# Modulation by chunks of features, streamed into four head tiles of the first projection

## The chip, the cores and the metric

The kernel runs on one core of one Trainium2 chip. The metric is the device time of one execution in microseconds (us); lower is better. The engines are named as in the profile: PE (TensorE, with PEld for its weight loads), DVE (VectorE), ACT (ScalarE), POOL (GpSimd) and SP (SyncE, which issues most DMAs).

## The reference, cut to what matters

Two networks run one after the other on 256 tokens of 1024 features, in float32. The change lies at the start of the first one, which has two layers. Each layer turns a conditioning vector into six modulation vectors (shift, scale and gate, twice), normalizes the tokens, shifts and scales them, projects them with `w_in` and attends in three kinds of heads:

```python
mod_x = (silu_c @ w_ada[l] + b_ada[l])[:, None, :]      # w_ada[l]: 1024 x 6144
mod_c = (silu_cc @ w_ada[l] + b_ada[l])[None, None, :]
sh1_x, sc1_x, gt1_x, sh2_x, sc2_x, gt2_x = jnp.split(mod_x, 6, axis=-1)
...
hx = modulate(rms_norm(x, g_norm1[l]), sh1_x, sc1_x)     # h * (1 + scale) + shift
hc = modulate(rms_norm(ctx, g_norm1[l]), sh1_c, sc1_c)
qa, ka, va, qb, kb, vb, qc, kc, vc = jnp.split(hx @ w_in[l], bounds, axis=-1)
...
oa, oa_t = mixer_a(...)   # grouped-query attention, rope
ob, ob_t = mixer_b(...)   # neighbourhood attention
oc, oc_t = mixer_c(...)   # differential attention, rope
x = x + gt1_x * (jnp.concatenate([oa, ob, oc], axis=-1) @ w_out[l])
```

The 256 context tokens go through the first layer beside the 256 tokens of `x`, so that a projection there has 512 columns. In the second layer the context only gives keys and values, and a query projection has 256 columns.

## The kernel before

Features lie on partitions, in eight chunks of 128 (`KC`), and tokens lie along the free dimension. A weight tile is 128 output features by all 1024 inputs, 512 KB. `weight` loads it into a `raw` buffer and splits it into `hi` (an ACT copy, L261) and `lo` (a DVE subtraction, L262); there are four buffers of each. A product of a chunk is three matmuls of 512 columns (`mm1`, L269 to L271), so that a projection tile is 24 matmuls. `gemm` runs the first tiles (its head, three of them) chunk by chunk side by side and the others one after the other. The accumulators are five PSUM banks (`mm`); three more (`at`) serve all else. `done` is called for each finished tile: for queries and keys it is the norm `qk` (a matmul at L450 with ACT and DVE work around it), for values a transpose (`values`, L468).

The modulation vectors come from `ada`, a generator. One step loads 512 KB of `w_ada` (128 inputs by one whole vector of 1024) into a `raw` buffer and adds it up with four matmuls (L372). Eight steps make a vector. `first` runs 16 steps, for the shift and scale of layer 0, before it loads the head's three weight tiles. After the eighth step come the norm's statistics (`stat_end`, L350 and L351, then the chain in `rsq`), and DVE multiplies the 16 half chunks of tokens with it (L820, L821). `mod_gain` (L413) makes the factors of all chunks at once, and `modulate` applies them: ACT writes the high part (L428), DVE the low one (L429, L430).

18 projection tiles follow in the order of `IN1`. `gemm` does the first six, three of them in its head. The other twelve are a generator, `project`. The attention calls `fill` once for each unit (a block of scores, its softmax and its transposes): it takes the next projection, or, when there is none left, an `ada` step for a later vector. The order of attention is c (differential), b (neighbourhood), a (grouped query). The framework sorts the instructions of each engine when the program is built; nothing is sorted on the chip.

Of the kernel before, what the change touches and what calls it, by code (L numbers as in the profile page):

```python
# [9 lines left out]
F32 = mybir.dt.float32  # L10
F32R = mybir.dt.float32r
# [27 lines left out]

_CON = [("ident", 128), ("ones", 128), ("ones128", 128), ("bd64", 128), ("bd32", 128), ("causal", 128)]  # L40
_COFF = {}
# [18 lines left out]
def _constants():  # L60
# [24 lines left out]
    put("winmask", np.where((kc[None] >= st[:, None]) & (kc[None] < st[:, None] + 16), 0.0, MASKED))  # L85
    put("causal", np.where(i[None, :] <= i[:, None], 0.0, MASKED))
    m = np.zeros((P, 8, P), np.float32)
    m[:, 0] = np.eye(P)
# [9 lines left out]
def prep(v):  # L98
# [13 lines left out]
    d["ccT"] = cc  # L112
    d["w_ada"] = f(v["w_ada"])

    def tiles(w):
# [70 lines left out]
class Kern:  # L186
# [91 lines left out]

    def gemm(self, tiles, done, head=3, hook=None, order=None, fill=None, ws=None):

# [135 lines left out]

    def modulate(self, l, v, gain, streams, zs, n, xn=None):

        nc = self.nc
        xs = []  # L420
        for c in range(KC):
            hi, lo = self.n(F32R), self.n(F32R)
            if xn:
                t = self.t()[:, :512]
                for part, _ in streams:
                    u = slice(part * 256, (part + 1) * 256)
                    g, sh = gain[:, c, part:part + 1], self.mod(l, v, c, part)
                    nc.scalar.activation(hi[:, u], xn[c][:, u], AF.Identity, scale=g, bias=sh)  # L428
                    nc.vector.tensor_scalar(t[:, u], xn[c][:, u], g, sh, ALU.mult, ALU.add)  # L429
                nc.vector.tensor_tensor(lo, t, hi.bitcast(F32), ALU.subtract)  # L430
                xs.append((hi, lo))
                continue
# [173 lines left out]
    def first_layer(self, l):  # L606
# [6 lines left out]
        both = ((0, X), (1, C))  # L613
        zs, head = None, self.head
        if not wc:
# [5 lines left out]
        cut = {n: [(h[:, :n], o[:, :n]) for h, o in xs] for n in (256, 512)}  # L621
        gains = {}
# [168 lines left out]
    def first(self, ctx):  # L791
# [19 lines left out]
        self.G1, self.G2 = {}, {}  # L811
        self.known, self.mods = -1, self.ada()
        for i in range(16):
            next(self.mods)
            if i == 7:
                with self.tc.issue_after(self.last_ada):
                    zs = [self.stat_end(s) for s in st]
                self.xn = [self.n() for _ in range(KC)]
                for c in range(KC):
                    nc.vector.tensor_tensor(self.xn[c][:, :256], self.H[:, c, TM:TH], zs[0], ALU.mult)  # L820
                    nc.vector.tensor_tensor(self.xn[c][:, 256:], self.C[:, c, :], zs[1], ALU.mult)  # L821
        self.head = [self.weight(A["w1_in"][0, j]) for j in range(3)]
        nc.sync.dma_start(self.CON1, A["con1"])
        nc.sync.dma_start(self.LAM, bass.AP(A["lamv"].tensor, 0, [[0, P], [1, 256]]))

# [465 lines left out]
def build(tc, A, out, dbg=None):  # L1291
    with ExitStack() as ctx:
# [7 lines left out]

_INS = ["hT", "cT", "ccT", "w_ada", "w1_in", "w1_out", "w1_up", "w1_dn", "w2_in", "w2_fg", "w2_out", "w2_up1", "w2_dn1",
        "w2_up2", "w2_dn2", "walpha", "vec", "lamv", "rpb", "con", "con1", "lmask"]
# [18 lines left out]
```

## Time and profile before

| | us |
|---|---|
| median of 3 runs | 2428.66 |
| fastest and slowest run | 2425.72, 2434.18 |
| the profiled execution's own time | 2433.39 |
| its span | 2431.6 |
| first projection matmul starts at | 43.10 |

Times in the rows are counted from the span's start. A row of a timeline gives start, duration, engine, line, operation, output<-input, count, and in brackets how long the engine was idle before and what ended that.

### The profile page before, as it was taken

What the parts mean: (1) busy time and instruction counts of PE and PEld (TensorE: products, weight loads), DVE (VectorE), ACT (ScalarE), POOL (GpSimd) and SP (SyncE); (2) the same over time, 40 slices, a digit from 0 to 9 for tenths busy, and PEclk for the clock granted to TensorE, in tenths of its full rate; (3) what the DMA queues carried; (4) which work ended last, traced back from release to release, by engine and by line L of the source; (5) the groups of instructions that cost most, each with busy time, mean ns of one, the idle gap of its engine ahead of it and who ended that gap; (6) DMA issues with size and microseconds to landing.
All of it is one profiled execution on the core that took longest, in us unless ns stands there. A gap on an engine that the chain in (4) does not pass through costs nothing. (4 is left out here: it accounts for less than half of the span.)

```text
span 2431.6 us, 40872 instructions
## 1 busy us (share of the span) xinstructions
PE 2320.8 (95%) x16128; PEld 2043.5 (84%) x16128; DVE 1523.2 (63%) x2605; ACT 1270.2 (52%) x2196; POOL 401.7 (17%) x417
## 2 busy tenths in 40 slices
PE   5999999999999989999999999899999999998998
PEld 3665677778877758999999988899989999888997
DVE  4667665444547776776664876676466557666664
ACT  3658644333346775664444545554454444466553
POOL 0300021000022001211111320321121122113111
PEclk8999999999999999999999999999999999999999
DMA  7313335433233246556555533445545545334653
GB/s 269 103 37 131 113 130 173 139 121 96 93 117 120 71 156 211 194 177 191 183 168 180 167 106 105 148 157 174 174 148 178 169 147 195 104 114 149 196 180 118
DMA packets 100993, 358.57 MB, mean 147 GB/s; under 512 B 11488, under 2 KB 12864, under 8 KB 100544
## 3 DMA queue, kind: packets, MB, share of 16 engines
q1 hardware_dynamic: 98640, 349.82, 44.4%
q0 software_dynamic: 1792, 5.53, 0.9%
q8 instruction: 127, 2.08, 0.4%
q10 hardware_dynamic: 368, 0.59, 0.1%
q14 instruction: 66, 0.54, 0.1%
HBM read 354.83 MB, written 1.07 MB: 146 GB/s over the span
## 5 line engine op out<-in xcount | busy, mean ns | idle before, releaser
L269 PE MATMUL mm_t<-n_t,hi_t 128*128 128x272 f32 (+2 forms) x3600 | 1112.4, 310 | 25.4 <-ACT n_t L839 18.7
L270 PE MATMUL mm_t<-n_t,hi_t 128*128 128x272 f32 (+2 forms) x3600 | 1109.5, 308 | 6.0 <-DVE n_t L840 5.0
L271 PE MATMUL mm_t<-n_t,lo_t 128*128 128x272 f32 (+2 forms) x3600 | 1106.0, 308 | 1.1 <-DVE lo_t L262 1.1
L262 DVE TENSOR_TENSOR lo_t<-raw_t,hi_t 128x1024 fp32r<-128x1024 f32 (+1 forms) x574 | 713.2, 1246 | 391.2 <-ACT hi_t L261 387.1
L261 ACT ACTIVATE hi_t<-raw_t 128x1024 fp32r<-128x1024 f32 (+1 forms) x574 | 595.5, 1039 | 680.6 <-PE mm_t L270 509.4
L269 PEld LDWEIGHTS mm_t<-n_t,hi_t 128*128 128x128 f32 x3600 | 686.0, 191 | 77.7 <-ACT n_t L839 20.9
L270 PEld LDWEIGHTS mm_t<-n_t,hi_t 128*128 128x128 f32 x3600 | 688.5, 191 | 38.1 <-DVE n_t L840 8.4
L271 PEld LDWEIGHTS mm_t<-n_t,lo_t 128*128 128x128 f32 x3600 | 687.9, 191 | 33.0 <-issue 5.8
L269 PE MATMUL mm_t<-q_t,hi_t 128*128 128x272 f32 (+2 forms) x896 | 274.6, 307 | 0.7 <-ACT q_t L306 0.7
L270 PE MATMUL mm_t<-q_t,hi_t 128*128 128x272 f32 (+2 forms) x896 | 274.4, 306 | 0.0
L271 PE MATMUL mm_t<-q_t,lo_t 128*128 128x272 f32 (+2 forms) x896 | 274.3, 306 | 0.0
L343 POOL TENSOR_TENSOR t_t<-t_t 128x272 f32<-128x272 f32 (+1 forms) x108 | 122.9, 1143 | 540.2 <-ACT t_t L339 515.2
L269 PEld LDWEIGHTS mm_t<-q_t,hi_t 128*128 128x128 f32 x896 | 168.4, 188 | 8.8 <-ACT q_t L306 1.1
L270 PEld LDWEIGHTS mm_t<-q_t,hi_t 128*128 128x128 f32 x896 | 168.9, 188 | 7.6 <-DVE q_t L307 0.2
L271 PEld LDWEIGHTS mm_t<-q_t,lo_t 128*128 128x128 f32 x896 | 168.9, 189 | 7.5
L888 POOL TENSOR_TENSOR t_t<-t_t 128x272 f32<-128x272 f32 (+1 forms) x88 | 75.6, 860 | 443.3 <-DVE t_t L882 386.9
L738 POOL TENSOR_TENSOR t_t<-t_t 128x512 f32<-128x512 f32 (+1 forms) x44 | 56.7, 1288 | 442.2 <-ACT t_t L737 442.2
L882 DVE TENSOR_TENSOR t_t<-mm_t,t_t 128x272 f32<-128x272 f32 (+1 forms) x176 | 75.6, 436 | 64.2 <-PE mm_t L271 62.4
L372 PE MATMUL at_t<-raw_t,CS 128*32 128x256 f32 x768 | 70.6, 431 | 35.7 <-DMA raw_t<-in_w_ada_dram 35.4
L307 DVE TENSOR_TENSOR q_t<-t_t,q_t 128x272 fp32r<-128x272 f32 (+2 forms) x112 | 55.8, 498 | 73.4 <-ACT q_t L306 73.4
L306 ACT ACTIVATE q_t<-t_t 128x272 fp32r<-128x272 f32 (+2 forms) x112 | 52.3, 467 | 90.4 <-POOL t_t L738 47.8
L480 ACT ACTIVATE t_t<-mm_t,s_t 128x512 f32<-128x512 f32 (+1 forms) x120 | 72.7, 607 | 26.5 <-DVE s_t L478 25.7
(253 smaller groups left out, 2146.9 us busy)
## 6 DMA issues: line engine op xcount, KB each, us to landing
raw_t<-in_w_up_dram SPq DMA_DIRECT2D x264, 512.0 KB, 3.3
raw_t<-in_w_in_dram SPq DMA_DIRECT2D x118, 512.0 KB, 3.4
raw_t<-in_w_ada_dram SPq DMA_DIRECT2D x96, 512.0 KB, 4.4
raw_t<-in_w_dn_dram SPq DMA_DIRECT2D x96, 448.0 KB, 3.3
raw_t<-in_w_dn_dram SPq DMA_DIRECT2D x48, 512.0 KB, 3.6
raw_t<-in_w_out_dram SPq DMA_DIRECT2D x32, 512.0 KB, 3.4
raw_t<-in_w_fg_dram SPq DMA_DIRECT2D x16, 512.0 KB, 3.3
q_t<-cum POOLq DMA_DIRECT2D x8, 272.0 KB, 7.4
```

The source lines that it names most:

```text
L261: nc.scalar.activation(hi[:, :k], raw[:, :k], AF.Copy)
L262: nc.vector.tensor_tensor(lo[:, :k], raw[:, :k], hi[:, :k].bitcast(F32), ALU.subtract)
L269: self.nc.tensor.matmul(ps, wh, xh, start=start, stop=False)
L270: self.nc.tensor.matmul(ps, wh, xl, start=False, stop=False)
L271: self.last_mm = self.nc.tensor.matmul(ps, wl, xh, start=False, stop=stop).ins
L307: self.nc.vector.tensor_tensor(lo, src, hi.bitcast(F32), ALU.subtract)
L343: st.eng.tensor_tensor(st.acc, st.acc, sq, ALU.add)
L372: self.last_ada = nc.tensor.matmul(ps[32 * g:32 * g + 32], self.CS[:, k, :], wv[:, g], start=k == 0, stop=k == KC - 1).ins
L480: nc.scalar.activation(pm[:, i * nk:(i + 1) * nk], sp[:, i * nk:(i + 1) * nk], AF.Exp, bias=m[:, i:i + 1], accum_out=sm[:, i:i + 1])
L738: nc.gpsimd.tensor_tensor(u, u, g, ALU.mult)
L882: nc.vector.tensor_tensor(u, ps, z[0], ALU.mult)
L888: nc.gpsimd.tensor_tensor(u, u, g, ALU.mult)
```

## The change

For layer 0 the shift and scale are no longer made as two whole vectors. The weights are packed again on the host (`w_ada0`) by chunks of 128 output features, each with its shift and scale columns together. `ada_chunk` loads a chunk in four DMAs of 256 KB into buffers of the `heads` pool (18 of them), adds up with eight matmuls (L433 of the changed kernel) and copies the sums to SBUF with ACT; `mod_chunk` adds the four partial sums with two small matmuls against a selector (L444), adds the bias, makes the gain of this chunk alone and writes its high and low part. `gemm` calls them through `feed`, so that the head's matmuls of chunk k follow chunk k's modulation. The head has four tiles, and their weights are loaded ahead of the modulation weights. The constants of rope and window are loaded after the last chunk, and the lambda vectors from ACT's queue. In both layers three more projections run before the first attention unit.

```diff
+    a = v["w_ada"][0, :, :2048].reshape(4, 2, P, 2, KC, P)
+    d["w_ada0"] = f(a.transpose(4, 0, 2, 1, 3, 5).reshape(KC, 4, P, 512))
...
         for i, k in enumerate(order):
+            if feed:
+                feed(k)
             for w, ps, t in zip(ws, pss, tiles):
                 self.mm1(ps, w, k, t[1][k], i == 0, i == KC - 1)
...
-        for l, v in ((l, v) for l in range(2) for v in range(6)):
+        for l, v in ((l, v) for l in range(2) for v in range(2 * (1 - l), 6)):
...
+    def ada_chunk(self, c):
+        nc = self.nc
+        ps = self.atp()[:, :256]
+        for h in range(2):
+            ws = [self.q()[:, :512] for _ in range(2)]
+            for i, w in enumerate(ws):
+                self.last_dma = nc.sync.dma_start(w, self.A["w_ada0"][c, 2 * h + i]).ins
+            for g in range(4):
+                self.last_ada = nc.tensor.matmul(ps[32 * g:32 * g + 32], self.CS[:, 4 * h + g, :],
+                                                 ws[g // 2][:, g % 2 * 256:(g % 2 + 1) * 256], start=h == 0, stop=h == 1).ins
+        e = self.t()[:, :256]
+        nc.scalar.activation(e, ps, AF.Copy)
+        return e
+
+    def mod_chunk(self, c, e):
+        nc = self.nc
+        m = self.atp()[:, :4].rearrange("p (v s) -> p v s", v=2)
+        for v in range(2):
+            nc.tensor.matmul(m[:, v], e[:, v * P:(v + 1) * P], self.con("sel"), start=v == 0, stop=v == 1)
+        o, _ = _VOFF["b_ada"]
+        for v in range(2):
+            nc.vector.tensor_scalar(self.MOD[0][:, v * KC + c], m[:, v], self.VEC[:, o + v * KC + c:o + v * KC + c + 1], None,
+                                    ALU.add)
+        gain = self.G1[0]
+        nc.vector.tensor_scalar(gain[:, c], self.MOD[0][:, KC + c], 1.0, self.gh[:, c:c + 1], ALU.add, ALU.mult)
...
-        xs = self.modulate(l, 0, self.G1[l], both, zs, 512, self.xn if wc else None)
+            def feed(k):
+                while len(sums) < min(k + 2, KC):
+                    sums.append(self.ada_chunk(len(sums)))
+                x = self.mod_chunk(k, sums[k])
...
-        self.gemm(tiles[:6], done, ws=head)
+        self.gemm(tiles[:6], done, ws=head, head=len(head), feed=feed,
+                  hook=late if wc else None)
...
+        for _ in range(3):
+            next(self.project)
         for j in range(2):
             po = self.attend(l, "c", get("qc", j), get("kc", j), get("vc", j), wc, lam=lam)
...
+        self.head = [self.weight(A["w1_in"][0, j]) for j in range(4)]
...
-        for i in range(16):
-            next(self.mods)
-            if i == 7:
-                with self.tc.issue_after(self.last_ada):
-                    zs = [self.stat_end(s) for s in st]
...
-        self.head = [self.weight(A["w1_in"][0, j]) for j in range(3)]
-        nc.sync.dma_start(self.CON1, A["con1"])
+        self.sums = [self.ada_chunk(c) for c in range(2)]
+        with self.tc.issue_after(self.last_ada):
+            zs = [self.stat_end(s) for s in st]
```

On PE, from the program's first matmul on, before: 16 modulation steps (here counted in matmuls), the statistics, then the head.

```order
L372 MATMUL at_t<-raw_t,CS 32x256 x32
L350 MATMUL at_t<-t_t,CON 128x256
L351 MATMUL at_t<-t_t,CON 128x256
L350 MATMUL at_t<-t_t,CON 128x256
L351 MATMUL at_t<-t_t,CON 128x256
L372 MATMUL at_t<-raw_t,CS 32x256 x32
L269 MATMUL mm_t<-n_t,hi_t 128x512
L270 MATMUL mm_t<-n_t,hi_t 128x512
L271 MATMUL mm_t<-n_t,lo_t 128x512
```

The same place on PE now (L433 is the chunk's sums, L444 the selector, L356 and L357 the statistics, L273 to L275 the head's matmuls).

```order
L433 MATMUL at_t<-q_t,CS 32x256 x16
L356 MATMUL at_t<-t_t,CON 128x256
L357 MATMUL at_t<-t_t,CON 128x256
L356 MATMUL at_t<-t_t,CON 128x256
L357 MATMUL at_t<-t_t,CON 128x256
L444 MATMUL at_t<-CON,t_t 128x2 x2
L433 MATMUL at_t<-q_t,CS 32x256 x8
L444 MATMUL at_t<-CON,t_t 128x2 x2
L433 MATMUL at_t<-q_t,CS 32x256 x8
L273 MATMUL mm_t<-n_t,hi_t 128x512
L274 MATMUL mm_t<-n_t,hi_t 128x512
L275 MATMUL mm_t<-n_t,lo_t 128x512
```

Four chunks' sums and two selectors stand ahead of the head's first matmul; the sums of the other four chunks and six selectors stand between its matmuls. The last of these, after the head's sixth chunk, on PE now:

```order
L275 MATMUL mm_t<-n_t,lo_t 128x512
L433 MATMUL at_t<-q_t,CS 32x256 x3
L444 MATMUL at_t<-CON,t_t 128x2 x4
L273 MATMUL mm_t<-n_t,hi_t 128x512 x4
L274 MATMUL mm_t<-n_t,hi_t 128x512
```

Between the selectors of the last two chunks and the matmuls of the seventh, nothing else stands on PE.

On DVE, around the tokens' multiplications with the norm, now (L447 adds the bias, L450 makes the gain, L456 is the first half of a low part): the first chunk's gain stands behind all 16 multiplications (L870, L871).

```order
L870 TENSOR_TENSOR n_t<-H,t_t 128x256
L871 TENSOR_TENSOR n_t<-C,t_t 128x256
L680 TENSOR_TENSOR lam_276<-s_t 128x1
L450 TENSOR_SCALAR gain_g_norm_0_253<-MOD_92,gh 128x2
L681 TENSOR_SCALAR lam_276<-lam_276 128x1
L447 TENSOR_SCALAR MOD_92<-at_t,VEC 128x2
L456 TENSOR_SCALAR t_t<-n_t,gain_g_norm_0_253,MOD_92 128x256 x2
```

Before, the same gain (L413) stood behind the whole of the modulation sums there.

On PE at the end of attention c in layer 0, before: the last projection, its norm (L450), transposes (L569), the weighted values (L579, L586), then the scores of attention b (L531).

```order
L271 MATMUL mm_t<-n_t,lo_t 128x512
L450 MATMUL at_t<-t_t,CON 128x512
L569 MATMUL at_t<-CON,t_t 128x128 x4
L579 MATMUL at_t<-n_t,q_t 64x256 x8
L586 MATMUL at_t<-n_t,q_t 64x256 x4
L531 MATMUL mm_t<-q_t 128x512 x2
```

The same place now (L483 norm, L561 scores of c, L602 transposes, L378 modulation sums for later vectors, L564 scores of b):

```order
L275 MATMUL mm_t<-n_t,lo_t 128x512
L561 MATMUL mm_t<-q_t 128x512 x2
L483 MATMUL at_t<-t_t,CON 128x512
L602 MATMUL at_t<-CON,t_t 128x128 x4
L378 MATMUL at_t<-raw_t,CS 32x256 x4
L561 MATMUL mm_t<-q_t 128x512 x2
L378 MATMUL at_t<-raw_t,CS 32x256 x4
L561 MATMUL mm_t<-q_t 128x256 x2
L378 MATMUL at_t<-raw_t,CS 32x256 x12
```

The last three units of c stand behind the last projection, with modulation steps between them, and the scores of b follow before the transposes of c's last two units.

## Rows read from the trace of the kernel before

**Rows 1.** The page, busy time of each engine: us, share of span, instructions.
```profile
PE 2320.8 (95%) x16128; PEld 2043.5 (84%) x16128; DVE 1523.2 (63%) x2605; ACT 1270.2 (52%) x2196; POOL 401.7 (17%) x417
```

**Rows 2.** Busy time by stretches: span start, PE, layer 0's attention, layer 1's.
```profile
core 0: us, PE busy (x) PEld busy (x) DVE busy (x) ACT busy (x) POOL busy (x), PEclk, DMA share, GB/s
...
43.10:48.40 5.30, 4.39 (x11) 3.13 (x11) 5.30 (x8) 4.91 (x8) 0.00 (x0) 0.55 0.97 334
48.40:62.50 14.10, 14.10 (x64) 11.64 (x62) 8.93 (x23) 6.57 (x12) 0.00 (x0) 1.00 0.32 115
...
82.40:192.50 110.10, 104.69 (x456) 72.47 (x456) 74.03 (x152) 68.94 (x142) 21.39 (x24) 0.98 0.18 53
192.50:199.50 7.00, 4.78 (x33) 2.48 (x32) 4.70 (x11) 6.64 (x14) 0.00 (x0) 1.00 0.00 0
199.50:279.00 79.50, 71.48 (x534) 44.10 (x534) 65.33 (x153) 71.11 (x166) 1.41 (x2) 0.98 0.54 186
762.50:832.00 69.50, 64.27 (x335) 45.32 (x334) 51.52 (x110) 47.81 (x96) 17.46 (x18) 1.00 0.31 99
832.00:870.00 38.00, 32.39 (x232) 26.00 (x228) 27.10 (x70) 32.95 (x73) 5.68 (x8) 0.92 0.09 25
```

**Rows 3.** Timeline of PE: statistics, last step, first projection; a later modulation stretch.
```profile
24.13 1.22 PE L350 MATMUL at_t<-t_t,CON 128*128 128x256 f32 x2
...
39.49 1.08 PE L372 MATMUL at_t<-raw_t,CS 128*32 128x256 f32 x8 [0.21 <-DMA raw_t<-in_w_ada_dram]
...
43.10 0.79 PE L269 MATMUL mm_t<-n_t,hi_t 128*128 128x512 f32 x1 [2.52 <-ACT n_t L428]
44.80 0.80 PE L270 MATMUL mm_t<-n_t,hi_t 128*128 128x512 f32 x1 [0.91 <-DVE n_t L430]
...
245.66 1.93 PE L372 MATMUL at_t<-raw_t,CS 128*32 128x256 f32 x32
```

**Rows 4.** Timeline of the start: SP's issues, and what waited for their landing.
```profile
3.40 27.97 SPq L369 DMA_DIRECT2D raw_t<-in_w_ada_dram  x16
6.78 0.42 ACT L339 ACTIVATE t_t<-H 128x256 f32<-128x256 f32 x1 [2.23 <-DMA H<-in_hT_dram]
...
12.41 2.27 PE L372 MATMUL at_t<-raw_t,CS 128*32 128x256 f32 x16 [12.41 <-DMA raw_t<-in_w_ada_dram]
...
16.13 1.08 PE L372 MATMUL at_t<-raw_t,CS 128*32 128x256 f32 x8 [0.17 <-DMA raw_t<-in_w_ada_dram]
```

**Rows 5.** Timeline of DVE and ACT: first and last of 16 multiplications, then the modulation.
```profile
28.70 0.42 DVE L820 TENSOR_TENSOR n_t<-H,t_t 128x256 f32<-128x256 f32 x1
...
34.66 0.41 DVE L821 TENSOR_TENSOR n_t<-C,t_t 128x256 f32<-128x256 f32 x1
...
41.54 0.18 DVE L381 TENSOR_TENSOR MOD<-t_t,VEC 128x16 f32<-128x16 f32 x1
41.75 0.17 DVE L413 SCALAR_TENSOR_TENSOR gain_g_norm<-MOD,s_t 128x16 f32<-128x16 f32 x1
41.95 1.09 ACT L428 ACTIVATE n_t<-n_t,MOD,gain_g_norm 128x256 fp32r<-128x256 f32 x2
```

**Rows 6.** Timeline of PE: a norm beside a projection; the end of attention c.
```profile
62.74 1.13 PE L450 MATMUL at_t<-t_t,CON 128*128 128x512 f32 x2
...
194.55 1.12 PE L450 MATMUL at_t<-t_t,CON 128*128 128x512 f32 x2 [1.62 <-ACT t_t L447]
...
196.05 1.95 PE L579 MATMUL at_t<-n_t,q_t 128*64 128x256 f32 x16
...
199.46 0.85 PE L531 MATMUL mm_t<-q_t 128*128 128x512 f32 x3 [0.60 <-ACT q_t L512]
```

**Rows 7.** Layer 1's attention b on PE's timeline; the page's group of weight conversions on ACT.
```profile
864.41 1.97 PE L551 MATMUL at_t<-CON,t_t 128*128 128x128 f32 x8 [3.09 <-ACT t_t L491]
866.31 3.64 PE L372 MATMUL at_t<-raw_t,CS 128*32 128x256 f32 x32
...
L261 ACT ACTIVATE hi_t<-raw_t 128x1024 fp32r<-128x1024 f32 (+1 forms) x574 | 595.5, 1039 | 680.6 <-PE mm_t L270 509.4
```

More of the change, by code (lines that the diff above doesn't have):

```diff
@@ L37 @@
 NVEC = _n
-_CON = [("ident", 128), ("ones", 128), ("ones128", 128), ("bd64", 128), ("bd32", 128), ("causal", 128)]
+_CON = [("ident", 128), ("ones", 128), ("ones128", 128), ("bd64", 128), ("bd32", 128), ("causal", 128), ("sel", 2)]
 _COFF = {}
@@ L86, in _constants @@
     put("causal", np.where(i[None, :] <= i[:, None], 0.0, MASKED))
+    put("sel", i[:, None] % 32 == np.arange(2)[None, :])
     m = np.zeros((P, 8, P), np.float32)
@@ L277, in mm, with gemm @@
             self.mm1(ps, w, k, xs[k], first and i == 0, last and i == len(xs) - 1)
-    def gemm(self, tiles, done, head=3, hook=None, order=None, fill=None, ws=None):
+    def gemm(self, tiles, done, head=3, hook=None, order=None, fill=None, ws=None, feed=None):
         order = order or range(KC)
@@ L415, in mod_gain, with modulate @@
         return a
-    def modulate(self, l, v, gain, streams, zs, n, xn=None):
+    def ada_chunk(self, c):
[22 more added lines that the diff above has]
+        nc.vector.tensor_scalar(gain[:, c], self.MOD[0][:, KC + c], 1.0, self.gh[:, c:c + 1], ALU.add, ALU.mult)
+        hi, lo, t, xn = self.n(F32R), self.n(F32R), self.t()[:, :512], self.xn[c]
+        for part in range(2):
+            u = slice(part * 256, (part + 1) * 256)
+            g, sh = gain[:, c, part:part + 1], self.mod(0, 0, c, part)
+            nc.scalar.activation(hi[:, u], xn[:, u], AF.Identity, scale=g, bias=sh)
+            nc.vector.tensor_scalar(t[:, u], xn[:, u], g, sh, ALU.mult, ALU.add)
+        nc.vector.tensor_tensor(lo, t, hi.bitcast(F32), ALU.subtract)
+        return hi, lo
+    def modulate(self, l, v, gain, streams, zs, n):
         nc = self.nc
@@ L422, in modulate @@
             hi, lo = self.n(F32R), self.n(F32R)
[L423 to L432, printed above, removed]
             for part, src in streams:
@@ L613, in first_layer @@
         both = ((0, X), (1, C))
-        zs, head = None, self.head
-        if not wc:
+        head, feed = self.head, None
+        cut = {256: [], 512: []}
+        if wc:
+            sums = self.sums
+            def feed(k):
+                while len(sums) < min(k + 2, KC):
+                    sums.append(self.ada_chunk(len(sums)))
+                x = self.mod_chunk(k, sums[k])
+                for n in cut:
+                    cut[n].append(tuple(a[:, :n] for a in x))
+        else:
             head = [self.weight(A["w1_in"][l, j]) for j in range(3)]
@@ L619, in first_layer @@
                 self.ada_step(l, 4)
-        xs = self.modulate(l, 0, self.G1[l], both, zs, 512, self.xn if wc else None)
-        cut = {n: [(h[:, :n], o[:, :n]) for h, o in xs] for n in (256, 512)}
+            for x in self.modulate(l, 0, self.G1[l], both, zs, 512):
+                for n in cut:
+                    cut[n].append(tuple(a[:, :n] for a in x))
         gains = {}
@@ L650, in first_layer, with late @@
         tiles = [(A["w1_in"][l, i], cut[n], n) for i, n in enumerate(ns)]
-        self.gemm(tiles[:6], done, ws=head)
+        def late():
+            with self.tc.issue_after(self.last_dma):
+                nc.sync.dma_start(self.CON1, A["con1"])
+        self.gemm(tiles[:6], done, ws=head, head=len(head), feed=feed,
+                  hook=late if wc else None)
         def project():
@@ L810, in first @@
             self.stat_add(st[1], self.C[:, c, :])
-        self.G1, self.G2 = {}, {}
-        self.known, self.mods = -1, self.ada()
-        for i in range(16):
-            next(self.mods)
-            if i == 7:
-                with self.tc.issue_after(self.last_ada):
-                    zs = [self.stat_end(s) for s in st]
[L818 to L821, printed above, removed]
-        self.head = [self.weight(A["w1_in"][0, j]) for j in range(3)]
-        nc.sync.dma_start(self.CON1, A["con1"])
-        nc.sync.dma_start(self.LAM, bass.AP(A["lamv"].tensor, 0, [[0, P], [1, 256]]))
+        self.sums = [self.ada_chunk(c) for c in range(2)]
+        with self.tc.issue_after(self.last_ada):
+            zs = [self.stat_end(s) for s in st]
+        self.xn = [self.n() for _ in range(KC)]
+        for c in range(KC):
+            nc.vector.tensor_tensor(self.xn[c][:, :256], self.H[:, c, TM:TH], zs[0], ALU.mult)
+            nc.vector.tensor_tensor(self.xn[c][:, 256:], self.C[:, c, :], zs[1], ALU.mult)
+        self.G1, self.G2 = {0: p1.tile([P, KC, 2], F32, name="gain_g_norm1_0")}, {}
+        self.gh = p1.tile([P, KC], F32, name="gh")
+        nc.vector.tensor_scalar(self.gh, self.vec(0, "g_norm1", 0, KC), -0.5, None, ALU.mult)
+        self.known, self.mods = 1, self.ada()
+        nc.scalar.dma_start(self.LAM, bass.AP(A["lamv"].tensor, 0, [[0, P], [1, 256]]))
         self.first_layer(0)
@@ L1298, in build @@
             k.second(c2)
-_INS = ["hT", "cT", "ccT", "w_ada", "w1_in", "w1_out", "w1_up", "w1_dn", "w2_in", "w2_fg", "w2_out", "w2_up1", "w2_dn1",
+_INS = ["hT", "cT", "ccT", "w_ada", "w_ada0", "w1_in", "w1_out", "w1_up", "w1_dn", "w2_in", "w2_fg", "w2_out", "w2_up1", "w2_dn1",
         "w2_up2", "w2_dn2", "walpha", "vec", "lamv", "rpb", "con", "con1", "lmask"]
```

## The prediction

> **What bounds the kernel now.** I read the page's busy times first: PE is busy 95% of the span, the next engine 63% [rows 1]. So the kernel is a long run of matmuls, and a change ahead of it counts only by what it does to the moments in which PE waits or does work that is not a projection. The largest such piece is the start, so I went to the timeline there. PE's first projection matmul starts at 43.10 us [rows 3]. Until then PE adds up modulation vectors as their weights land, and waits. Behind the last step (39.49, 1.08 us long) the bias, the gain and the first high part still have to be made: bias at 41.54, gain at 41.75, ACT from 41.95 to 43.04 [rows 5], and PE starts 0.06 us later. From there on PE is the bound for a while: in 43.1 to 48.4 it executes 11 matmuls at a mean granted clock of 0.55, so mostly at the lower of its two levels, and then 64 in 14.1 us, 0.22 us each, without a gap [rows 2]. Last I read the attention stretches. In attention c of layer 0 PE is busy 104.69 of 110.10 us; in b and a behind it ACT is busy 71.11 of 79.50 [rows 2]. There ACT sets the pace, and PE has room. Layer 1 is alike: PE 64.27 of 69.50 us in c, then ACT 32.95 of 38.00.
>
> The profiled execution took 2433.39 us for a span of 2431.6 us; it is 4.7 us above the median of the three runs, 2428.66. The sum below is a difference of moments within the span. I add it to the median. A measurement of this kernel tells about 0.3%, 7.3 us, from no change.
>
> **The start, step by step.**
>
> *When the head can begin.* The first transfers keep their order. Between the landing of H (6.78) and that of the fourth modulation step (16.13) [rows 4] there come C, two tables of constants and four steps, by their shapes 3.85 MB in 9.35 us, or 0.41 MB per us. The change puts four weight tiles, 2.1 MB, where those four steps were, so they have landed at about 16.1. Two chunks of 1.05 MB then end at 21.2, and the statistics may start once their sums are done, about 0.9 us later: 22.1, where it was 24.13 [rows 3]. The statistics' chain and the 16 multiplications are the same work: from 24.13 to the end of the last one (34.66 + 0.41) it took 10.94 us. The first chunk's gain now stands behind them on DVE. Some small operations on lambda are between, 0.5 us as I take it from the 0.17 of a small operation [rows 5]. From gain to first matmul it was 43.10 - 41.75 = 1.35. Together 22.1 + 10.94 + 0.5 + 1.35 = 34.9. **Term A: 34.9 - 43.1 = -8.2.** Bounds: -9.1 if the chunks' sums hide wholly behind their landing, -5.8 if the stream runs a tenth slower and the sums run at the lower clock.
>
> The transfers after that do not matter: at 2.55 us per chunk the last of eight lands near 37, while the head is in its first chunk. Eighteen buffers hold four and a half chunks, and four chunks' sums stand ahead of the head, so the rest can be issued before 30. The wait on the last transfer holds back the constants of the rope and SP's next weight tiles behind them. They have from 37 to about 68 to land, so I cost it at nothing; if that cover were gone, PE would wait for one 512 KB tile, 1.24 us by the spacing of the steps in [rows 4] ((16.13 - 12.41) / 3). ACT issues the lambda transfer while it waits for its first input anyway. The four conversions of the head's weights move ahead of the statistics, where ACT and DVE are waiting; the copies of the chunks' sums to SBUF, and the low parts, take less of ACT and DVE per chunk than PE's 12 matmuls.
>
> *What now stands between the head's matmuls.* Half of the modulation sums: before, all 16 steps were done before 43.1; now four chunks (eight steps' worth) are not. Back to back, 32 records (four steps) take 1.93 us [rows 3], so four chunks take 3.9. **Term B: +3.9** (3.4 to 5.1; the upper end is the 0.64 us of an isolated step). It is not hidden, because PE is the bound there. The selectors are new: twelve matmuls for the last six chunks, float32 and so two records each. No row has one; the nearest above is the 16 records of L579, 1.95 us or 0.12 each, with 256 columns where the selector has two, and below, it may cost little more than nothing. Because a full 128-column weight load remains, I take the upper row. **Term C: 24 x 0.12 = +2.9** (0.6 to 4).
>
> *A wait that is new.* Mostly a chunk's selector is followed by the next chunks' sums, which cover bias, gain and high part. Before the seventh chunk of the head nothing covers it. From the bias (41.54) to PE (43.10) it took 1.56; with a second chunk's bias in DVE's queue and less the other selector about 1.9. Behind it queue the head's last 24 matmuls and thus the first norms. **Term D: +1.9** (0 to 4.2, the latter if the clock falls over it).
>
> The slow first 5.3 us of the head come again, only earlier, as PE was waiting ahead of it in both: nothing. The fifth tile's buffers come free as the head's first tile ends, 10 matmuls or 2.3 us before the head's end, and its conversion takes 1.04 on ACT [rows 7]: hidden. The fourth tile was read before behind the head, with one norm's 1.13 us [rows 6] in it; that norm now comes later, on the same engine: no term.
>
> Start together: -8.2 + 3.9 + 2.9 + 1.9 = **+0.5** (-5.1 to +7.5). The head start is spent on PE itself.
>
> **Attention three projections later.** Layer 0: the same twelve projections come before the same ACT-bound stretch. At the end of c, PE waits 1.62 us for a norm's square and 0.60 for ACT before b [rows 6], and in 192.5 to 199.5 it is busy 4.78 of 7.0 us [rows 2]. Now c's last three units are without a projection between them and b's first scores are pulled among them. This can win at most the 2.2 us, and lose one wait like the 1.62 for each of the units, 4.9. ACT is busy 6.64 of those 7 us, so ACT can gain little. **Term E: -1** (-2.2 to +4.9).
>
> Layer 1: its units are fewer, and four of the twelve projections ran in b, beside a busy ACT. Three of these, query tiles of 256 columns, leave that stretch: 3 x 24 x 0.11 (half of 0.22) = 7.9 us of PE that was partly free now lies where PE is the bound. In return ACT loses three conversions (3 x 1.04) and three norms of five passes from a stretch that it bounds at 87%; with the conversions alone it is 3.6 us given back, and with the norms, at about 0.35 us for each of 15 passes (an estimate, a little below the 0.42 us of a 256-column pass in [rows 4]), 5.3 / 0.87 = 6 us more. **Term F: 0** (-1.7 to +4.3). PE's 3.09 us wait for ACT and the following 3.64 us of sums at the lower clock (1.93 at the upper) [rows 7, 3] may come or go with the order.
>
> Sum: 0.5 - 1 + 0 = -0.5, so 2428.66 - 0.5 = **2428**.
>
> **Two rules.** The head now alternates with sums and transfers. The Trainium skill (TensorE: Matmul & The Clock Gate, HAM oscillation) describes kernels in which each K tile waits for its DMA longer than it computes, and starts at the lower clock every time. In this kernel the last transfers land near the head's first chunk by the sum above, so the rule's case should not arise; what it would cost is a rival below. The skill (DMA: Bandwidth & Descriptors, Rules for kernel authors) also asks for 1 MiB per DMA or more, and these go from 512 KB to 256 KB. No run so far shows 256 KB transfers in a full queue, and the 512 KB ones follow each other at 1.24 us; a slower stream is the last rival.
>
> **The rivals.**
>
> *Faster.* The selectors and the new wait cost next to nothing (C 0.6, D 0), A and B are at their best ends: -9.1 + 3.4 + 0.6 = -5.1; with E at -2.2 and F at -1.7, -9.0: 2420. For it speaks that a two-column matmul may be far cheaper than 0.12 us per record; against it that all must go well. Chance 0.22.
>
> *Slower, by attention.* The units without a projection between them leave PE in waits like those of 1.62 and 3.09 us, and the tiles that were free beside ACT are paid: E +4.9 and F +4.3 with the start's +0.5 make +9.7: 2438. It decides where ACT's saved passes do not shorten the stretch by about 6 us. Against it: ACT is near full there. Chance 0.16.
>
> *Slower, by the clock.* PE stays at the lower level through the head. The same 32 records take 3.64 us there and 1.93 at the upper, a factor of 1.9, so the 85 matmuls that ran at the upper level gain 85 x 0.22 x 0.9 = 16.8 us: 2445. Chance 0.04.
>
> *The stream of smaller transfers is slower.* At half the rate (5.1 us per chunk) the second chunk lands 5 us later and the head begins at 40, and the last chunk lands at 57, some 10 us before the head's end: it costs about 5 us, 2433, still within 0.3%. Chance 0.06.
>
> **How the numbers follow.** My own case, terms near the values taken, 0.52, gives 2428 with 2421.5 to 2436 around it. The outer cases pull to 2420 and 2438 to 2445; leaving out the clock case and the tails, the range is 2417 to 2440. Faster by over 0.3%: the faster case, 0.22. Slower: 0.16 + 0.04 and 0.01 of the stream's, 0.21. The rest, 0.57, is within 0.3%.
>
> **What would show it.** In the changed kernel's trace: the statistics near 22, the first head matmul near 35, the fourth tile's end near 68 (34.9 + 5.3 + 85 x 0.22 + 8.7 = 67.6; before, 43.1 + 5.3 + 85 x 0.22 + 1.1 = 68.2); sums between the head's matmuls at about 1 us per chunk; one wait of about 2 us before the seventh chunk, on ACT's high part. If the first matmul is later than 38, the stream or the statistics were misjudged; if the head ends before 65, terms B to D were too dear. The first scores of b should come about 192 to 199, and w_out's first matmul near 279. Wrong would make it a clock that stays low past the first 5 us, or b's units in either layer waiting longer on ACT than before.

## The result and the profile after

The changed kernel takes 2450.48 us (median of 4 runs, 2448.73 to 2454.03), beside 2428.28 for the kernel before (4 runs, 2425.72 to 2434.18): ratio 1.009, 95% interval 1.0068 to 1.0111. It is slower by about 22 us; forecast were 2428, 2417 to 2440. The profiled execution took 2449.93 us for a span of 2448.1, which is 16.5 us longer than the span before. Five of the 22 us stand between the kernel before's profiled execution (2433.39) and its median; the 16.5 can be placed.

PE's timeline of the start, changed kernel (L433 sums of a chunk, L444 selector, L356 and L357 statistics, L273 to L275 projection, L483 norm):

```profile
19.57 5.26 PE L433 MATMUL at_t<-q_t,CS 128*32 128x256 f32 x32 [19.57 <-DMA q_t<-in_w_ada_dram]
24.76 0.70 PE L356 MATMUL at_t<-t_t,CON 128*128 128x256 f32 x2
...
35.90 0.80 PE L273 MATMUL mm_t<-n_t,hi_t 128*128 128x512 f32 x1 [5.62 <-ACT n_t L455]
...
43.60 0.50 PE L444 MATMUL at_t<-CON,t_t 128*128 128x2 f32 x4
44.03 1.07 PE L433 MATMUL at_t<-q_t,CS 128*32 128x256 f32 x16
45.03 0.61 PE L444 MATMUL at_t<-CON,t_t 128*128 128x2 f32 x4
45.57 1.05 PE L433 MATMUL at_t<-q_t,CS 128*32 128x256 f32 x10
46.55 0.97 PE L273 MATMUL mm_t<-n_t,hi_t 128*128 128x512 f32 x3
...
61.50 0.63 PE L433 MATMUL at_t<-q_t,CS 128*32 128x256 f32 x6
62.06 1.23 PE L444 MATMUL at_t<-CON,t_t 128*128 128x2 f32 x8
64.86 2.08 PE L273 MATMUL mm_t<-n_t,hi_t 128*128 128x512 f32 x4 [1.57 <-ACT n_t L455]
66.74 0.63 PE L274 MATMUL mm_t<-n_t,hi_t 128*128 128x512 f32 x1
67.17 0.63 PE L275 MATMUL mm_t<-n_t,lo_t 128*128 128x512 f32 x1
...
73.24 1.02 PE L483 MATMUL at_t<-t_t,CON 128*128 128x512 f32 x2
```

The head begins 7.2 us earlier than in [rows 3]. Sums and selectors interrupt it three times, and before the seventh chunk PE waits 1.57 us for ACT's high part. Behind that wait matmuls follow each other at 0.43 us instead of 0.23. The windows of the same kernel show the granted clock there:

```profile
55.90:61.40 5.50, 5.50 (x25) 4.36 (x24) 1.57 (x5) 1.09 (x2) 0.00 (x0) 1.00 0.01 3
61.40:64.90 3.50, 1.91 (x16) 1.23 (x15) 1.88 (x9) 1.56 (x4) 0.00 (x0) 0.87 0.01 2
64.90:71.20 6.30, 6.30 (x16) 4.97 (x17) 1.75 (x4) 0.96 (x3) 0.00 (x0) 0.53 0.00 0
...
201.10:301.60 100.50, 84.72 (x566) 52.22 (x565) 73.61 (x176) 80.12 (x192) 0.00 (x0) 0.92 0.38 131
```

The four tiles end at 73.2. In the kernel before the fifth tile's first matmul is at 68.97, with one norm's 1.1 us already done; so the start loses 4.3 + 1.1 = 5.4 us. The fifth tile's first matmul in the kernel before, in the changed kernel, and in e11, a run below whose edit leaves the start of the kernel before as it was:

```profile
68.97 0.39 PE L269 MATMUL mm_t<-n_t,hi_t 128*128 128x512 f32 x1
```

```profile
73.69 0.79 PE L273 MATMUL mm_t<-n_t,hi_t 128*128 128x512 f32 x1
```

```profile
66.24 0.39 PE L269 MATMUL mm_t<-n_t,hi_t 128*128 128x512 f32 x1
```

In e2, which also leaves that start alone, it is at 67.55. So the kernel before was profiled in an execution with a slow start, in which the last modulation weights came 2.3 to 3.3 us later than in e2 and e11. Against these two the changed start loses 6.8 and 8.1 us and not 5.4; that would account for 1.4 to 2.7 of the five us above.

One delay lies ahead of all modulation work. The tokens (H) are waited for until 9.34, where it was 6.78 [rows 4]:

```profile
0.74 0.40 ACTq L876 DMA_DIRECT2D LAM<-in_lamv_dram  x1
6.01 0.42 ACT L858 ACTIVATE CS<-t_t 128x256 f32<-128x256 f32 x1 [3.56 <-DMA t_t<-in_ccT_dram]
9.34 0.42 ACT L345 ACTIVATE t_t<-H 128x256 f32<-128x256 f32 x1 [1.61 <-DMA H<-in_hT_dram]
```

The load of the lambda vectors, which the change moved to ACT's queue, is the only transfer issued ahead of H that the kernel before doesn't have there. All thirteen runs with it land H between 9.1 and 9.3 us, the three without it (the kernel before, e2, e11) between 6.3 and 6.8. No run takes it out alone, so that it is the cause is likely but not shown; every variant with the chunked start carries this delay of 2.6 us or more.

The last of the windows above answers to 199.50:279.00 in [rows 2]: from b's first score to w_out's first matmul it was 79.5 us and is 100.5. ACT, which sets the pace there, is idle for 20.4 us of it (100.5 - 80.12) where it was idle for 8.4 (79.5 - 71.11); the other 9 us are ACT's work for c's last units, which now lies inside this stretch.

As a mark that all variants share I use w_out's first eviction on DVE. Before, and then in the changed kernel:

```profile
304.86 0.48 DVE L704 SCALAR_TENSOR_TENSOR H<-mm_t,MOD,H 128x256 f32<-128x256 f32 x1 [9.12 <-PE mm_t L271]
```

```profile
322.45 0.48 DVE L757 SCALAR_TENSOR_TENSOR H<-mm_t,MOD,H 128x256 f32<-128x256 f32 x1 [8.47 <-PE mm_t L275]
```

So 17.6 us are lost by then, 5.4 in the start and about 12 behind it, in layer 0's attention. In layer 1 the last such eviction is 17.0 us late (933.51, now 950.46): nothing more is lost there. What ACT waited for in the stretch 201 to 302 of the changed kernel (total, times, longest):

```profile
ACT t_t L524 <- DVE s_t L521: 8.7, 8, 1.8
ACT n_t L312 <- PE at_t L619: 4.2, 5, 2.0
ACT t_t L513 <- DVE s_t L511: 3.0, 4, 1.6
ACT t_t L513 <- DVE MOD L387: 2.8, 1, 2.8
```

It waits for the reciprocal of its own sums (L521), for weighted values, for the maximum ahead of an exponential, and once, for 2.8 us, for the end of a modulation vector on DVE (L387).

### The profile page after: what moved, and what is told of

Same layout as the page of the kernel before. It is cut to its first block, busy times and chain, and to the rows that moved or that the text cites. A ratio compares the mean times of both kernels' runs of the same rounds, so it can differ in the third digit from the quotient of the medians.

```text
span 2448.1 us, 40992 instructions
## 1 busy us (share of the span) xinstructions
PE 2331.2 (95%) x16160; PEld 2051.6 (84%) x16160; DVE 1529.3 (62%) x2624; ACT 1271.6 (52%) x2202; POOL 399.4 (16%) x417
## 3 DMA queue, kind: packets, MB, share of 16 engines
q8 instruction: 127, 2.08, 0.3%
## 5 line engine op out<-in xcount | busy, mean ns | idle before, releaser
L273 PE MATMUL mm_t<-n_t,hi_t 128*128 128x272 f32 (+2 forms) x3600 | 1113.2, 311 | 29.8 <-ACT n_t L891 18.7
L275 PE MATMUL mm_t<-n_t,lo_t 128*128 128x272 f32 (+2 forms) x3600 | 1105.8, 307 | 1.1 <-DVE lo_t L266 1.1
L273 PEld LDWEIGHTS mm_t<-n_t,hi_t 128*128 128x128 f32 x3600 | 685.8, 191 | 80.9 <-ACT n_t L891 20.9
L275 PEld LDWEIGHTS mm_t<-n_t,lo_t 128*128 128x128 f32 x3600 | 687.6, 191 | 32.6 <-issue 5.2
L273 PE MATMUL mm_t<-q_t,hi_t 128*128 128x272 f32 (+2 forms) x896 | 274.6, 307 | 0.7 <-ACT q_t L312 0.7
L275 PE MATMUL mm_t<-q_t,lo_t 128*128 128x272 f32 (+2 forms) x896 | 274.5, 307 | 0.0
L273 PEld LDWEIGHTS mm_t<-q_t,hi_t 128*128 128x128 f32 x896 | 168.5, 188 | 8.5 <-ACT q_t L312 1.1
L275 PEld LDWEIGHTS mm_t<-q_t,lo_t 128*128 128x128 f32 x896 | 168.6, 188 | 7.7
L511 DVE TENSOR_REDUCE s_t<-mm_t 128x1 f32<-128x512 f32 (+1 forms) x100 | 67.5, 678 | 7.6 <-PE mm_t L561 4.9
```

What stands on the lines that cost most here:

```text
L273: self.nc.tensor.matmul(ps, wh, xh, start=start, stop=False)
L275: self.last_mm = self.nc.tensor.matmul(ps, wl, xh, start=False, stop=stop).ins
L511: nc.vector.tensor_reduce(m, sp.rearrange("p (s k) -> p s k", s=nseg), AX.X, ALU.max, negate=True)
```

## The experiments

In each, "mark" is the start of w_out's first eviction less 304.86, from one profiled execution. That execution can lie off the median: those of e11, e12 and e14 are the fastest of their runs, 6.0, 7.3 and 4.7 us below the median. "Stretch" is from b's first score to w_out's first matmul. Ratios are to the kernel before, with 95% intervals.

**Parts undone or done alone.** e1 takes the three early projections out, e3 leaves them in layer 1 only, e2 adds them to the kernel before.

e3's edit (e1 has no such loop, and e2 has the old one):

```diff
         order = []
-        for _ in range(3):
+        for _ in range(0 if wc else 3):
             next(self.project)
```

> The changed kernel without the three projections ahead of attention, in both layers; the chunks and the four head tiles stay. Theory (the loss is mostly layer 0's attention without a projection beside it): the stretch from the first score of b to w_out's first matmul is again near 80 us and the kernel is near 2428 + 5 = 2433 to 2438. Rival (the chunked start leaves a worse order behind it, whoever comes first): the stretch stays near 95 us and the time stays near 2450.

> The changed kernel with the three early projections in layer 1 only. Theory (layer 0 pays, layer 1 neither pays nor gains): like the run without any early projection, within 3 us of it. Rival (part of the loss is layer 1's): more than 4 us above that run.

> The kernel before with the three projections ahead of attention as the only edit, in both layers. Theory: about 12 us slower than before, 2438 to 2443, with the loss between the last projection and w_out's first matmul of layer 0. Rival (the chunked start is the cause): the time of before, 2425 to 2431.

Measured: e1 1.0058 (1.0036 to 1.0079), mark +11.1, stretch 79.9 us. e3 1.0043 (1.0026 to 1.0061), mark +9.9, stretch 79.4. e2 1.0045 (1.0029 to 1.0061), mark +13.1, stretch 101.6. Without early projections in layer 0 the stretch is back at its old length; with them alone it is as long as in the changed kernel. Layer 1's make no difference that can be told. But e1 and e3 are slower than the 2433 to 2438 that I gave for e1: the chunked start costs some 10 us of mark without early projections, not 5. e3's PE timeline shows a part of it, behind the sixth tile:

```profile
86.71 1.13 PE L483 MATMUL at_t<-t_t,CON 128*128 128x512 f32 x2 [1.41 <-ACT t_t L480]
89.21 2.08 PE L561 MATMUL mm_t<-q_t 32*128 32x512 f32 x4 [1.38 <-DVE q_t L491]
```

These are two waits for the norms ahead of c's first scores, which follow on the lower clock (2.08 us for the four; 1.13 in the kernel before, at 82.40). In the changed kernel a projection covered them. From the fifth tile's first matmul to these scores e3 takes 3.4 us more than the kernel before. So the early projections also win something, and lose more.

**The head's wait.** e4 makes each chunk's modulation one chunk ahead; e8 does the same without early projections in layer 0.

```diff
-                x = self.mod_chunk(k, sums[k])
-                for n in cut:
+                while len(cut[256]) < min(k + 2, KC):
+                    i = len(cut[256])
+                    x = self.mod_chunk(i, sums[i])
```

> The changed kernel with each chunk's selector, bias, gain and high part issued one chunk ahead of its matmuls, so that matmuls of the chunk before cover them. Theory (the wait of 1.57 us before the seventh chunk and the lower clock behind it cost 4.5 us, the sums and selectors 8.6): the fourth tile ends near 69 instead of 73.2, and the kernel is near 2446. Rival (the granted clock falls anyway, after the selectors and sums): no wait, but matmuls of 0.42 us spacing again behind some chunk, the fourth tile's end at 71.5 or later.

> Two edits on the changed kernel: no early projections in layer 0, and each chunk's selector, bias, gain and high part one chunk ahead of its matmuls. Theory (what is left of the loss, ratio 1.0043, is waits of 1.57, 1.41 and 1.38 us in the start and behind it, each pair with some 6 us at the lower clock): the fourth tile ends near 70, the waits behind the sixth tile stay, ratio 1.002 to 1.003. Rival (the four tiles' norms pile up on ACT whenever the head ends): what PE gains in the head it waits for behind it, ratio 1.004 again.

Measured: e4 1.0083 (1.0061 to 1.0104), e8 1.0049 (1.003 to 1.0068). In both the wait is gone, and in e4 the fourth tile ends at 69.9, as the theory says. Its time hardly follows: mark +16.0 instead of +17.6. In e8 the rival is right: behind the head PE waits 1.45 and 3.06 us for the norms, mark +9.0 beside e3's +9.9. In e4 the gain goes mostly in another place. PE waits for ACT ahead of the same transposes in both kernels; e4's row, then the windows 148:155 of e4 and of the changed kernel:

```profile
146.68 0.66 PE L501 MATMUL at_t<-CON,t_t 128*128 128x128 f32 x4 [1.14 <-ACT t_t L498]
```

```profile
148.00:155.00 7.00, 7.00 (x17) 5.04 (x17) 3.43 (x9) 2.78 (x11) 0.00 (x0) 0.53 0.25 77
```

```profile
148.00:155.00 7.00, 5.88 (x31) 4.19 (x29) 4.67 (x11) 5.62 (x15) 0.67 (x1) 1.00 0.19 53
```

The changed kernel's wait there was 1.12 us long (at 150.50), and its clock stayed up.

**What the early projections take away.** With three projections taken early, c's last three units have none beside them and take modulation steps instead. e5 keeps the early projections and leaves c's first three units empty, so that its last ones have projections again; e6 takes no steps in c; e9 is e5 with steps added in c's last three units; e7 takes two projections early; e11 is e5's edit on the kernel before.

e5 and e11 (`self.skip` is 3 ahead of c):

```diff
     def fill(self, l):
+        if l == 0 and self.skip:
+            self.skip -= 1
+            return
         if next(self.project, None) is None:
             self.ada_step(l, 4)
```

e9, where `skip` counts on below zero and reaches -7 at the tenth of c's twelve units:

```diff
+        if l == 0 and self.skip > 0:
+            self.skip -= 1
+            return
+        if l == 0:
+            self.skip -= 1
-        if next(self.project, None) is None:
+        if next(self.project, None) is None or (l == 0 and self.skip < -6):
             self.ada_step(l, 4)
```

e6 (`self.ready` becomes true behind c, in layer 1 at once), and e7:

```diff
-        if next(self.project, None) is None:
+        if next(self.project, None) is None and self.ready:
             self.ada_step(l, 4)
...
-        for _ in range(3):
+        for _ in range(2 if wc else 3):
             next(self.project)
```

> The changed kernel, its three early projections kept, but in layer 0 the first three units of attention c get no projection beside them, so that the last one gets one again. In the order of its instructions five to six units' scores then stand ahead of b's first transposes, as in the kernel before; in the changed kernel two do. Theory (layer 0 loses because ACT's next exponential waits for scores that are issued one unit late): from b's first score to w_out's first matmul near 80 us again, not 95, and the kernel 1.004 to 1.006 of before. Rival (three units without a projection beside them cost, wherever they stand): the stretch may shorten, but c grows by as much, and the ratio stays near 1.009.

> The changed kernel, but where layer 0's attention c has run out of projections it takes no modulation step; all 24 steps then run beside b and a, as before the change. In the order of its instructions still two units' scores stand ahead of b's first transposes. Theory (the scores' order): the stretch of b and a stays at 93 to 98 us and the ratio near 1.009. Rival (the modulation steps that move into c, their transfers and PSUM tile, upset b): near 80 us, ratio 1.004 to 1.006.

> The changed kernel with two projections ahead of layer 0's attention instead of three (layer 1 keeps three). In the order four units' scores stand ahead of b's first transposes, where it is six with none and two with three; over the first thirty sets of transposes the mean is 3.9, against 5.2 and 3.0. Theory (the scores' order sets the loss): the stretch of b and a lies between, 84 to 92 us, and the ratio near 1.006 to 1.008. Rival (only whether c's end has a projection counts): near 95 us, ratio near 1.009.

> The run with the first three units of c left without a projection (e5), and in c's last three units a modulation step beside the projection. With e5, e6 and the changed kernel this makes a square: a projection at c's end or none, modulation steps there or none. Measured so far by w_out's first eviction against 304.86 before: projection and no step +6.7, neither +10.6, steps alone +17.6. Theory now (steps in c cost only where no projection stands beside them, since PE then issues b's scores late and waits): within 2 us of e5, ratio 1.003 to 1.004. Rival (a step in c costs by itself, 7 us for three): w_out's first eviction at +13 to +14, ratio 1.006.

> The kernel before with three early projections, and no projection beside the first three units of layer 0's attention c; nothing of the chunked start. Theory (early projections cost only by what they take away from c's end): the stretch of b and a near 80 us, w_out's first eviction within 2 us of 304.86, ratio 0.999 to 1.001. Rival (they cost by themselves): the stretch longer than 85 us or c longer by as much, ratio 1.003 or more, as with the early projections alone (1.0045).

Measured ("behind the head" is how much longer it takes from the fifth tile's first matmul to the mark than the 235.89 us of the kernel before):

| | ratio (interval) | mark | behind the head | stretch | ACT idle in it |
|---|---|---|---|---|---|
| e5: projections at c's end, no steps | 1.0032 (1.0021 to 1.0043) | +6.7 | +3.0 | 79.8 | 8.4 |
| e9: projections and steps | 1.0049 (1.003 to 1.0067) | +9.5 | +7.9 | 87.6 | 12.8 |
| e6: neither | 1.0043 (1.0032 to 1.0055) | +10.6 | +6.6 | 93.6 | 12.8 |
| changed kernel: steps alone | 1.009 (1.0068 to 1.0111) | +17.6 | +12.9 | 100.5 | 20.4 |
| e7: two early | 1.0054 (1.0032 to 1.0075) | +12.7 | +11.0 | 96.4 | 19.8 |
| e11: e5 on the kernel before | 1.0015 (1.0001 to 1.0028) | -1.2 | +1.6 | 80.4 | 8.9 |

The windows of this stretch in e5, and in e9:

```profile
206.00:285.80 79.80, 72.09 (x535) 44.51 (x535) 65.42 (x154) 71.44 (x166) 1.41 (x2) 0.98 0.54 185
```

```profile
205.90:293.50 87.60, 76.38 (x525) 47.58 (x523) 68.71 (x160) 74.76 (x176) 2.31 (x2) 0.94 0.42 142
```

e5's row is that of [rows 2] again, each number within 0.7 us, and e11 shows the same without the chunks. So the early projections by themselves cost little: 3.6 us by e11's ratio, which lies above the 0.999 to 1.001 that the theory gave, and 1.6 by its trace, counted behind the head (its mark of -1.2 is owed to a start 2.7 us faster than in the trace of the kernel before). What costs is that c's end loses its projections to modulation steps: of the changed kernel's +17.6, 10.9 are this, or 9.9 of the 12.9 behind the head.

The four kernels e5, e9, e6 and the changed one make a square. Counted behind the head, the lost projections cost 3.6 us without steps in c (e6 against e5) and 5.0 with them (changed kernel against e9); the steps cost 4.9 beside projections and 6.3 without. The marks alone would give 3.9 and 8.1, 2.8 and 7.0, but a good part of this gap is the head: in e9 its clock did not fall (last section), and it ended 2 us earlier than in e5, ahead of anything that e9's edit changes. So both cost. That each is worse beside the other is not shown: the difference of 1.4 us is less than one trace tells, and by the ratios it is within the intervals.

My theory of how ACT comes to wait, that b's scores are issued too few units ahead, did not hold. e5's stretch came as it says, with a ratio a little better than its 1.004. But with four units ahead (e7) the stretch should have been 84 to 92 us and was 96.4; e7's ratio is below both answers, as its head's clock did not fall. With two ahead but no steps in c (e6) the stretch of 93.6 is the theory's, but the ratio of 1.0043 is the rival's. In e9 the mark and the ratio lie between the two answers that I had allowed.

**Where the steps fall.** e13 keeps the three steps in c and gives b's first three units none, so that from the fourth on each stands at its old unit.

(`self.skip` is 0 ahead of c.)

```diff
         if next(self.project, None) is None:
+            if l == 0:
+                self.skip += 1
+                if 3 < self.skip <= 6:
+                    return
             self.ada_step(l, 4)
```

> The changed kernel, but b's first three units take no modulation step, so that from b's fourth unit on every step stands at the unit at which it stood before the change; the three steps in c stay. If the steps cost by where they fall within b and a: like the run without steps in c (e6), w_out's first eviction near +10.6, ratio 1.004 to 1.005. If they cost by standing in c, where no projection covers their transfers: near +17.6, ratio 1.008 to 1.009.

Measured: 1.0043 (1.0028 to 1.0058), mark +12.3, stretch 92.7, ACT idle 13.9. By the ratio it is e6, by the mark 1.7 us more. So of the steps' 7.0 us about 5 (4.6 behind the head) come with the steps of b and a standing three units ahead, or with their running on without a break from c's end into b, which e13 doesn't tell apart; little comes from their standing in c. ACT's single wait of 2.8 us for a modulation vector's end is probably part of it: the changed kernel, e2 and e4 have it, and e6, e7 and e13 do not.

**A better start.** e10 joins e5 and e4. e12 is e5 with all eight chunks' sums ahead of the head. e14 is e10 with three head tiles.

```diff
-                while len(sums) < min(k + 2, KC):
+                while len(sums) < KC:                                       # e12
...
-        self.head = [self.weight(A["w1_in"][0, j]) for j in range(4)]
+        self.head = [self.weight(A["w1_in"][0, j]) for j in range(3)]       # e14
```

> e5 (the three early projections, no projection beside the first three units of c) and e4 (each chunk's selector, bias, gain and high part one chunk ahead) together. If the two gains are apart, as their places are: the fourth tile ends near 70, w_out's first eviction near 308, ratio 1.001 to 1.002. If the three microseconds of the head are lost again behind it, as in e4 and e8: ratio 1.003, like e5.

> e5, but with the sums of all eight chunks ahead of the head's first matmul, so that only selectors stand in it. If the sums between the head's matmuls cost what a row says (four chunks, 3.9 us) and the first matmul comes about when the last chunk has landed and been summed (39 to 41 instead of 35.9): the fourth tile's end moves by -1 to +1 us from 73, ratio 1.003 like e5. If the sums are dearer there than 3.9, or the wait of 1.57 us goes with them: the fourth tile ends near 70, ratio 1.002. If the transfers end later than 40: later than 74, ratio 1.004 or more.

> e10 with three head tiles instead of four, 72 matmuls in the head instead of 96; the fourth tile is read behind the head, as before the change. If the four tiles' norms pile up on ACT behind the head and cost there: ratio 1.000 to 1.001, and shorter waits on ACT between 70 and 130 us. If a head of 72 matmuls covers the chunks' chain (bias, gain, high part) less well: waits inside the head, ratio 1.003 or more. If neither matters: 1.002, like e10.

Measured: e10 1.002 (1.0009 to 1.003), mark +5.6; e14 1.0014 (1.0006 to 1.0023), mark +3.0; e12 1.0044 (1.003 to 1.0058), mark +2.7. e10's fourth tile ends at 69.9 and not, as e5's, at 72.2; of these 2.3 us 1.1 are left at the mark. By the ratio it stands at the upper end of what was expected if the gains are apart; the mark was expected near 308 and is 310.4. In e14 PE waits 1.2 us in all between 70 and 130, in e10 3.5. That would fit four tiles' norms piling up, but the kernel before, with three head tiles, waits 3.3 there, and the two intervals overlap: it is not shown. Neither beats the kernel before, and both carry the late H. e12 stays open: in its trace the fourth tile ends at 68.6, better than any answer given, while its ratio is that of the worst; its profiled execution, 2436.77 us, was the fastest of seven with a median of 2444.11, so its trace doesn't stand for its time. That trace's head is of interest all the same (from 36 to its first matmul at 43.3, and the 4.7 us from there on):

```profile
36.00:43.30 7.30, 6.59 (x50) 3.49 (x48) 2.17 (x13) 1.48 (x3) 0.00 (x0) 1.00 1.03 399
43.30:48.00 4.70, 4.70 (x26) 4.00 (x25) 4.70 (x15) 3.51 (x8) 0.00 (x0) 1.00 0.39 155
```

PE had been summing until then, and the head's first 4.7 us run at the upper level; the kernel before had 0.55 there [rows 2], behind a wait.

## Why the prediction was wrong

- **Term A** (-8.2): -7.2, and only -4.9 and -3.9 against the starts of e2 (head at 40.79) and e11 (39.79). The sum took its 43.1 from an execution nearly 5 us above the median and added the difference to the median, without asking where in the span those 5 us lay. On the other side the statistics began at 24.76, not 22.1, because the second chunk's sums ended at 24.7. "The first transfers keep their order" failed: the lambda load, which the sum put at nothing, stands ahead of them, H landed 2.6 us later, and the first modulation weights were waited for until 19.57, where the sum had 16.1 + 0.6. The statistics' chain won 1.6 us back.
- **Terms B and C** (+6.8): 8.4. The three interruptions last 2.95, 3.62 and 3.36 us, less the wait of 1.57. Four records of a selector stand 0.54 us apart from what follows, 0.13 each, so the row taken for C (0.12) was right; the sums' 64 records at 0.063 make 4.0 and the selectors' 24 make 3.1, and the other 1.2 us lie at the changes from one kind to the other.
- **Term D** (+1.9, upper end 4.2 "if the clock falls over it"): the wait came at its place, on ACT's high part, with 1.57 us, and the clock did fall: 15 matmuls in 6.3 us, which take 3.4 at 0.227, so 2.9 more. Together 4.5: just above the upper end. e4 removes both and ends the head 3.3 us earlier. The wait alone doesn't decide the fall: e7 and e9 have the same 1.57 us there and no fall (below).
- **Start together** (+0.5): +5.4, with the fourth tile's end at 73.2 and not 67.6: 1.0 of A, 1.6 of B and C, 2.6 of D (these sum to 0.3 too much). The bound of +7.5 held it; against e11's start, with +8.1, it would not have.
- **Term E** (-1, upper end +4.9) is the main step that failed. It costed c's end alone, with one wait for each unit, and took "the same ACT-bound stretch" behind it as given. That stretch grew by 12 us of idle ACT and a granted clock of 0.92 instead of 0.98, and the mark moved by about 12 beyond the head. e5 and e11 show that the early projections as such are not the cause, e6, e9 and e13 that c's missing projections and the displaced modulation steps are. The rival "slower by attention" had the right side, and less than half the price.
- **Term F** (0): layer 1 adds -0.6 between the marks of the two layers, and e3 against e1 nothing that can be told.
- **The rivals of the start.** The stream of 256 KB transfers was a little slower: from 24 to 40 us it moved 374 to 393 GB/s, where 404 to 410 were moved ahead of it, and a chunk took 2.7 us and not 2.55. A window ahead of them, and the one in which they moved the least:

```profile
12.00:18.00 6.00, 0.00 (x0) 0.00 (x0) 5.09 (x21) 6.00 (x17) 4.61 (x6) 1.00 1.03 404
24.00:30.00 6.00, 5.45 (x54) 3.61 (x52) 2.87 (x11) 3.00 (x8) 0.00 (x0) 1.00 1.02 374
```

No matmul of the head waited for a DMA. The Trainium skill (DMA: Bandwidth & Descriptors, Rules for kernel authors) asks for 1 MiB per DMA; here transfers of a quarter of that ran 3 to 9% below the larger ones ahead of them. Nor did the case of the Trainium skill (TensorE: Matmul & The Clock Gate, HAM oscillation) arise, a DMA wait before each K tile: the head's clock fell once, behind a wait for ACT.

What stays open is the path by which the missing projections at c's end and the displaced steps make ACT idle throughout b and a. ACT waits 8.7 us for the reciprocals of its own sums, beside 5.8 in the kernel before. That could mean that too few independent units are in its queue, but the number of scores issued ahead doesn't foretell it.

## What to carry to other kernels

An edit that only pulls work ahead takes it away from somewhere. Ask which stretch loses its filler, and cost everything up to the next barrier, not the moment at which the filler is missing. The stretch that ACT bound at 90% depended in its length on how the instructions were interleaved: fillers taken out or moved to other units cost some 10 us here with the work unchanged, and that shows in ACT's idle time and in TensorE's granted clock, not in ACT's busy time. And where all streams of a start end in the same engine, starting it earlier moves the hidden sums onto it: 7.2 us won at the front were 8.4 us of sums and selectors in the head. Look, too, at where a profiled execution differs from the median before a moment of it enters a sum, and at what stands ahead of the first input: a load of 128 KB placed there went with 2.6 us of delay in every run that had it.

## What the runs showed of the hardware

A single wait of 1.1 to 1.6 us on PE, with work at the upper level before it, may be followed by 3 to 7 us at the lower level, or may not. In the head the wait of 1.57 us stands at the same place in eight of the kernels. In the changed kernel and in e1, e3, e5, e6 and e13 the clock fell behind it; in e7 and e9 it stayed up. e9's rows of PE there, 0.23 us apart where the changed kernel's were 0.43:

```profile
66.52 0.39 PE L274 MATMUL mm_t<-n_t,hi_t 128*128 128x512 f32 x1
66.75 0.39 PE L275 MATMUL mm_t<-n_t,lo_t 128*128 128x512 f32 x1
66.97 0.39 PE L274 MATMUL mm_t<-n_t,hi_t 128*128 128x512 f32 x1
```

The 24 matmuls behind that wait took 5.6 us in e7 and e9, 6.9 to 7.1 in e1, e3, e5, e6 and e13, and 8.4 in the changed kernel. A fall thus cost 1.3 to 2.9 us, about as much as the wait or more. So the trace of one execution tells a cost of that size only roughly, and a gain in waits can be lost again by a fall elsewhere, as in e4.
